# One pad for all pools, and the seven operands of the FFN's products at seven distances from the weights

## The chip, the cores and the metric

The kernel runs on one core of a Trainium2 chip. The metric is the device time of one execution in microseconds, the median of several runs. Profiled executions are looked at on the same core; times inside them count from the first instruction.

## What is computed

One layer of a streaming encoder on 512 tokens of width 1024, all in float32. A combined projection feeds three mixers and their gates, the gated branches are added and projected, and a gated feed-forward network (FFN) follows. The change touches memory placement in all of it, and code in the FFN alone:

```
D_MODEL, SEQ = 1024, 512
D_FF = 2816                       # 22 blocks of 128

h = rms_norm(x, norm_mix)
proj = h @ w_in                   # pool, LRU, q, k, v, three gates
...
merged = g0 * (y_pool @ w_branch[0]) + g1 * (y_lru @ w_branch[1]) + g2 * (y_sb @ w_branch[2])
x = x + merged @ w_out
h2 = rms_norm(x, norm_ffn)
act = silu(h2 @ w_ffn_gate) * (h2 @ w_ffn_up)
x = x + act @ w_ffn_down
```

## The kernel before

Every float32 product is made of three matmuls of a reduced-precision type (`float32r`): each operand is split into a high part (ScalarE copies it into the narrower type) and a low part (VectorE subtracts the high part from the original), and TensorE adds high x high, high x low and low x high (`mm3`, lines 215 to 218). A weights' chunk is loaded by a DMA issued on SP, split by `split_w` (lines 89 to 93) into tiles `whi` and `wlo`, three buffers each, and then used. TensorE loads 128x128 weights for every matmul, ahead of it, and streams the other ("moving") operand past them, 512 or 256 columns at a time.

The stages, with the tiles that the prediction names:

- gates, LRU and the q, k, v products: the moving operand of `half_chunk` (lines 264 to 272) is the normalised input `HH`, `HL`, in the pool `hp` on the right-hand side of the memory; in `tok_product` (line 654) the roles are exchanged, and `HH`, `HL` (or differences of them, on the left-hand side) are the weights
- the attention, whose tasks are dealt out between the matmuls of pool and branch chunks. Its products with 256 and 384 columns are `z` (scores) and `py` (lines 216 to 218 again)
- the output projection `ps_out`; its moving operand `mth`, `mtl` lies in the pool `cor`, on the right-hand side
- the FFN. Two of the eleven column chunks of gate and up are made directly (`ps_fg`, `ps_fu`). For the other nine, `seven(c)` replaces eight half-size products by seven (`product`, lines 1113 to 1121, matmuls at line 1119, 256 columns wide): the weights' blocks and their sums are named 11, 12, S2, S1, S3, S4, 22, and each goes with one of seven operands made from the activations: 11, 21, T2, T1, T3, 22, T4 (the table `WITH`). `split_b` (line 1040) makes an operand's high and low tile, `B0...`
- the down projection. Chunks kc = 4 to 10 of the activations are multiplied directly into `ps_d` (the loop with `split_act`, from line 1228); chunks 0 to 3 go through the seven products again, with operands `B1...`, made by `split_b` and `split2` (line 1204), into `ps_dy` and `ps_dx`

A pool's tiles with one tag share that tag's buffers in turn: a new tile waits until the last reader of the tile before it in the same buffer is done. In the FFN's pool `gp`, the tag "g" has 27 buffers of 4 KB per partition (`GBUFS`). They hold the eleven `act` tiles, the temporaries `tx`, `ty`, the split activations `ah`, `al`, sums, and the fourteen high and low tiles of the seven operands. Tiles of the constants' pool `cst` come first in memory, and the pools on the left-hand side follow it, so the size of `cst` shifts all of them.

The scheduler of the language orders the instructions of each engine from priorities and its own estimates; background tasks (`bg`) are emitted one by one between groups of matmuls.

Of the kernel before, what the change touches and what calls it, by code (L numbers as in the profile page):

```python
# [8 lines left out]
F32 = mybir.dt.float32  # L9
F32R = mybir.dt.float32r  # L10
# [6 lines left out]
P = 128  # L17
S = 512
# [7 lines left out]
QSCALE = float(HD) ** -0.5  # L26
NEG = -1.0e30
WARM = 8
GBUFS = 27
NDIRECT = 2  # L30
KD = 4
H = S // 2
AHEAD = 200
NAW, NAT, NAB = 8, 8, 13
NSP = 44
NLD = 12
# [24 lines left out]
def layer_kernel(ctx: ExitStack, tc: tile.TileContext, x, xt, vecs, w_in, w_pool, w_rg, w_ig,  # L61
# [5 lines left out]
    cst = ctx.enter_context(tc.tile_pool(name="cst", bufs=1))  # L67
# [131 lines left out]
    def emit_next():  # L199
# [4 lines left out]
        key, make = specs[i]  # L204
        with tc.high_priority(AHEAD if i > 3 else 0):
            ready[key] = make(str(i))
# [16 lines left out]
    def vcol(name, i=0):  # L223
        o = VOFF[name] + i
        return vt[:, o:o + 1]

    warm = cst.tile([P, S], BF16, tag="warm", name="warm")
    dve.memset(warm, 1.0)
    idn = cst.tile([P, P], F32, tag="idn", name="idn")
# [719 lines left out]
    for c in range(4):  # L949
        merge(2, c, chan_chunk(("br", 2, c), ysb_hl), g2[c])  # L950
        mth, mtl = corner([2, S], f"mth{c}", F32R), corner([2, S], f"mtl{c}", F32R)
        for j in range(2):
            h, l = mth[:, j, :], mtl[:, j, :]
# [7 lines left out]
    with ExitStack() as ffn:  # L961
        gp = ffn.enter_context(tc.tile_pool(name="gp", bufs=GBUFS))
        fp = ffn.enter_context(tc.tile_pool(name="fp", bufs=4, space=PSUM))

        def g4(shape, name, dt=F32):

            return gp.tile([P] + shape, dt, tag="g", name=name)
# [13 lines left out]
        for c in range(4):  # L981
# [5 lines left out]
            for j in range(2):  # L987
                k = 2 * c + j
                if c % 2 == 0:
                    x1p[c // 2, j] = mp.tile([P, 2, S], F32, tag="m", name=f"x1{c}{j}")  # L990
                t = x1p[c // 2, j][:, c % 2, :]
# [37 lines left out]
        B = {}  # L1029

        def norm2(k):
            for j in range(2):
                b = BN.setdefault((k // 4, j), None)
                if b is None:
# [2 lines left out]
                dve.scalar_tensor_tensor(b[:, k % 4, :], x1[k][:, js], vcol("norm_ffn", k),  # L1037
                                         rb2[:, js], ALU.mult, ALU.mult)

        def split_b(nm, key, which=0):  # L1040
            h, l = g4([4, H], f"B{which}{nm}h", F32R), g4([4, H], f"B{which}{nm}l", F32R)
            act(h, BN[key], AF.Copy)
            dve.tensor_tensor(l, BN[key], h.bitcast(F32), ALU.subtract)
            B[which, nm] = h, l
# [5 lines left out]
        def prepare_b():  # L1050
            nrm = [lambda k=k: norm2(k) for k in range(8)]
            return nrm[:4] + [lambda: split_b("11", (0, 0))] + nrm[4:] + [
                lambda: split_b("21", (1, 0)),
                lambda: diff_b("T1", (0, 1), (0, 0)),
                lambda: diff_b("T2", (1, 1), "T1"),
                lambda: split_b("T2", "T2"),
                lambda: split_b("T1", "T1"),
                lambda: diff_b("T3", (1, 1), (0, 1)),
                lambda: split_b("T3", "T3"),
                lambda: split_b("22", (1, 1)),  # L1060
                lambda: diff_b("T4", (1, 0), "T2"),
                lambda: split_b("T4", "T4")]
# [125 lines left out]
        for m in range(4):  # L1188
            t = fp.tile([P, 2, S], F32, tag="mm", name=f"ps_d{m}")
# [3 lines left out]
        def ablk(i, j):  # L1193
            return [acts[2 * i + n][:, :, j * H:(j + 1) * H] for n in range(2)]
# [7 lines left out]
            return [t[:, 0:2, :], t[:, 2:4, :]]  # L1202

        def split2(nm, i, j):
            h, l = g4([4, H], f"B1{nm}h", F32R), g4([4, H], f"B1{nm}l", F32R)
            for n, src in enumerate(ablk(i, j)):
                ns = slice(2 * n, 2 * n + 2)
                act(h[:, ns, :], src, AF.Copy)
                dve.tensor_tensor(l[:, ns, :], src, h[:, ns, :].bitcast(F32), ALU.subtract)
            B[1, nm] = h, l  # L1210

        todo = [lambda: load_a(DOWN), lambda: load_a(DOWN + 1),
                lambda: split2("11", 0, 0),
                lambda: split2("21", 1, 0),
                lambda: diff2("T1", ablk(0, 1), ablk(0, 0)),
                lambda: split_b("T1", "T1", 1),
                lambda: diff2("T2", ablk(1, 1), halves(BN["T1"])),
                lambda: split_b("T2", "T2", 1),
                lambda: diff2("T3", ablk(1, 1), ablk(0, 1)),
                lambda: split_b("T3", "T3", 1),  # L1220
                lambda: split2("22", 1, 1),
                lambda: diff2("T4", ablk(1, 0), halves(BN["T2"])),
                lambda: split_b("T4", "T4", 1)]
# [4 lines left out]
        for kc in range(KD, last + 1):  # L1228
            split_act(kc + 1)
            ah, al = split.pop(kc)  # L1230
            for e in range(2):
# [3 lines left out]
                for j in range(4):  # L1235
# [5 lines left out]
                    if kc == last:  # L1241
                        t = x1[m]
# [64 lines left out]
```

## Time and profile before

| | us |
|---|---|
| median of 3 runs | 957.63 (956.97 to 958.15) |
| the profiled execution | 956.69 |
| its span, first to last instruction | 954.9 |
| TensorE (PE) busy in the span | 941.5 |
| VectorE (DVE) busy | 703.5 |
| ScalarE (ACT) busy | 493.7 |

The granted clock of TensorE is 0.999 of full speed over the span. a tile's buffer number is left out of its name; PEld is the load of weights, which overlaps the matmul before it. [...] The chain of work that ended last is followed back from the last instruction; where TensorE is never idle, it is simply TensorE's own order. Instructions of VectorE and ScalarE on 128x1024 elements take 1.22 and 1.06 us, and follow each other at 1.14 and 0.95.

### The profile page before, as it was taken

The numbers are of one execution on the slowest core, as the hardware profiler recorded it, in microseconds if no ns is written. First come the engines' busy times: TensorE is split into PE (matmuls) and PEld (weight loads), VectorE is DVE, ScalarE is ACT, GpSimd is POOL, SyncE is SP. The second block draws the span as 40 slices with busy tenths as digits, with TensorE's granted clock in tenths as the row PEclk, the third lists the DMA queues.
The fourth block names the chain that finished last, engine by engine and source line by source line (L and its number), as shares of the span: only waits on it lengthen the run. The fifth ranks groups of instructions, "written<-read, shape, count | busy, mean of one in ns | idle before, by whom it ended". The sixth has DMA issues, their size and how long they took to land.

```text
span 954.9 us, 13025 instructions
## 1 busy us (share of the span) xinstructions
PE 941.5 (99%) x5090; PEld 802.7 (84%) x5090; DVE 703.5 (74%) x876; ACT 493.7 (52%) x664; POOL 43.1 (5%) x71
## 2 busy tenths in 40 slices
PE   8899999999999999999999999999999999999998
PEld 5787778788888888788788878889999999988898
DVE  6597677978696599865865554699888887787464
ACT  5567779445755466654543223555555555652232
POOL 1100000131121000000000000000000000000000
PEclk9999999999999999999999999999999999999999
DMA  8474343661713933165432234345533334523001
GB/s 269 138 260 130 111 136 129 199 204 58 224 65 138 297 117 121 63 178 165 146 101 88 89 114 153 108 122 145 150 93 89 111 95 129 166 98 111 1 27 63
DMA packets 127790, 124.12 MB, mean 130 GB/s; under 512 B 7280, under 2 KB 107632, under 8 KB 127728
## 3 DMA queue, kind: packets, MB, share of 16 engines
q1 hardware_dynamic: 123840, 109.13, 36.9%
q0 software_dynamic: 3888, 14.16, 4.4%
q8 instruction: 40, 0.66, 0.3%
q14 instruction: 22, 0.18, 0.1%
HBM read 107.01 MB, written 16.25 MB: 129 GB/s over the span
## 4 chain that ended last, share of the span: by engine, by line
PE 91%; DVE 5%; ACT 2%; DMA 1%; issue 1%; SPq 0%; POOL 0%; DVEq 0%; ACTq 0%; POOLq 0%
PE ps_y L1119 11%; PE ps_q L654 9%; PE ps_x L1119 8%; PE ps_br L216 4%; PE ps_br L218 4%; PE ps_br L217 4%; PE ps_gate L217 4%; PE ps_gate L218 4%; PE ps_gate L216 4%; PE ps_d L216 3%; PE ps_d L218 3%; PE ps_d L217 3%; PE ps_dy L1119 2%; PE ps_dx L1119 2%; PE ps_out L216 2%; PE ps_lru L217 2%
## 5 line engine op out<-in xcount | busy, mean ns | idle before, releaser
L92 ACT ACTIVATE whi<-raw 128x1024 fp32r<-128x1024 f32 x93 | 98.3, 1058 | 159.0 <-PE ps_br L217 44.8
L93 DVE TENSOR_TENSOR wlo<-raw,whi 128x1024 fp32r<-128x1024 f32 x93 | 113.6, 1221 | 78.7 <-ACT whi L92 74.2
L1109 ACT ACTIVATE wh_S<-w_S 128x1024 fp32r<-128x1024 f32 x44 | 46.6, 1061 | 58.7 <-PE ps_y L1119 27.2
L1110 DVE TENSOR_TENSOR wl_S<-w_S,wh_S 128x1024 fp32r<-128x1024 f32 x44 | 53.6, 1221 | 13.7 <-ACT wh_S L1109 13.6
L1109 ACT ACTIVATE wh<-w 128x1024 fp32r<-128x1024 f32 x33 | 35.0, 1060 | 50.8 <-issue 13.4
L93 DVE TENSOR_TENSOR wlo<-qw,whi 128x1024 fp32r<-128x1024 f32 x36 | 43.9, 1221 | 20.5 <-ACT whi L92 20.2
L1110 DVE TENSOR_TENSOR wl<-w,wh 128x1024 fp32r<-128x1024 f32 x33 | 40.3, 1222 | 18.9 <-ACT wh L1109 18.9
L92 ACT ACTIVATE whi<-qw 128x1024 fp32r<-128x1024 f32 x36 | 38.0, 1056 | 30.4 <-PE ps_q L654 17.1
L216 PE MATMUL ps_gate<-HH,whi 128*128 128x512 f32 x128 | 50.9, 397 | 0.0
L218 PE MATMUL ps_gate<-HH,wlo 128*128 128x512 f32 x128 | 50.8, 397 | 0.0
L217 PE MATMUL ps_gate<-HL,whi 128*128 128x512 f32 x128 | 50.7, 396 | 0.0
L216 PE MATMUL ps_d<-ah,whi 128*128 128x512 f32 x112 | 43.6, 391 | 0.0
L217 PE MATMUL ps_d<-al,whi 128*128 128x512 f32 x112 | 43.6, 389 | 0.0
L218 PE MATMUL ps_d<-ah,wlo 128*128 128x512 f32 x112 | 43.6, 389 | 0.0
L1097 DVE TENSOR_TENSOR w_S<-w,w 128x1024 f32<-128x1024 f32 x22 | 26.9, 1222 | 3.4 <-PE ps_d L217 2.9
L218 PEld LDWEIGHTS ps_gate<-HH,wlo 128*128 128x128 f32 x128 | 24.1, 188 | 5.8
L217 PEld LDWEIGHTS ps_gate<-HL,whi 128*128 128x128 f32 x128 | 24.1, 188 | 5.7
L216 PEld LDWEIGHTS ps_gate<-HH,whi 128*128 128x128 f32 x128 | 24.1, 188 | 5.6
L1097 DVE TENSOR_TENSOR w_S<-w,w_S 128x1024 f32<-128x1024 f32 x22 | 26.9, 1223 | 0.6
L872 DVE TENSOR_TENSOR_SCAN E<-K,zero 128x511 f32<-128x511 f32 (+3 forms) x32 | 25.5, 813 | 1.5 <-ACT K L867 1.3
L216 PE MATMUL ps_out<-mth,whi 128*128 128x512 f32 x64 | 25.4, 398 | 0.9 <-DVE g L299 0.9
L216 PE MATMUL ps_gate<-hu,whi 128*128 128x512 f32 x64 | 25.2, 394 | 1.0 <-ACT whi L366 0.7
(638 smaller groups left out, 3047.8 us busy)
## 6 DMA issues: line engine op xcount, KB each, us to landing
raw<-in_w_in_dram SPq DMA_DIRECT2D x39, 512.0 KB, 4.1
qw<-in_w_in_dram SPq DMA_DIRECT2D x24, 512.0 KB, 4.6
raw<-in_w_branch_dram SPq DMA_DIRECT2D x24, 512.0 KB, 3.4
w<-in_w_ffn_gate_dram SPq DMA_DIRECT2D x36, 256.0 KB, 3.5
w<-in_w_ffn_up_dram SPq DMA_DIRECT2D x36, 256.0 KB, 4.2
raw<-in_w_ffn_down_dram SPq DMA_DIRECT2D x14, 512.0 KB, 3.5
qd<-r POOLq DMA_DIRECT2D x12, 512.0 KB, 3.4
at<-qd SPq DMA_DIRECT2D x24, 256.0 KB, 5.2
```

What stands on the lines that cost most here:

```text
L92: act(hi, raw, AF.Copy)
L93: dve.tensor_tensor(lo, raw, hi.bitcast(F32), ALU.subtract)
L216: nc.tensor.matmul(ps, lh, rh, start=start, stop=False, skip_group_check=skip)
L217: nc.tensor.matmul(ps, lh, rl, start=False, stop=False, skip_group_check=skip)
L218: nc.tensor.matmul(ps, ll, rh, start=False, stop=stop, skip_group_check=skip)
L654: nc.tensor.matmul(ps[:, a, :], b_[:, k, ts_], a_[:, kk, :], start=first and n == k == 0, stop=n == 2 and k == 3, skip_group_check=True)
L872: dve.tensor_tensor_scan(E[:, f - 1:c0 + n - 1][:, ::-1], K[:, f:c0 + n][:, ::-1], zero[:, 0:1].to_broadcast([P, c0 + n - f]), 1.0, ALU.mu ...
L1097: dve.tensor_tensor(t, raw[c, x], raw[c, y], op)
L1109: act(h, raw[c, nm], AF.Copy)
L1110: dve.tensor_tensor(l, raw[c, nm], h.bitcast(F32), ALU.subtract)
L1119: nc.tensor.matmul(o, a[:, w, k, :], b[:, k, :], start=first and n == k == 0, stop=n == 2 and k == 3, skip_group_check=True)
```

## The change

A tile of 104 floats (416 B per partition) that nothing uses is added to `cst`. The seven operands get a tag each in `gp`, with one buffer that is used by `B0...` and then by `B1...`; high and low part lie in one tile of 8448 B, at an offset that is chosen per operand. "g" keeps 13 buffers. The offsets are such that each operand starts at the named number of bytes past the starts of the weights, modulo 512 B: 4 for 11, 256 for 21, 16 for T2, 320 for T1, 48 for T3, 384 for 22, 128 for T4.

```diff
-GBUFS = 27
+GBUFS = 13
...
+PAD = 104
...
+    cst.tile([P, PAD], F32, tag="pad", name="pad")
     warm = cst.tile([P, S], BF16, tag="warm", name="warm")
...
+        DIST = {"11": 4, "21": 256, "T2": 16, "T1": 320, "T3": 48, "22": 384, "T4": 128}
+        order = list(DIST)
+
+        def operand(which, nm):
+            n = order.index(nm)
+            o = (DIST[nm] - 256 * (n % 2)) // 4
+            assert 0 <= o <= 64
+            t = gp.tile([P, 2 * S * 2 + 64], F32R, tag="B" + nm, name=f"B{which}{nm}", bufs=1)
+            return [t[:, o + i * 1024:o + (i + 1) * 1024].rearrange("p (k t) -> p k t", k=4)
+                    for i in range(2)]
+
         def split_b(nm, key, which=0):
-            h, l = g4([4, H], f"B{which}{nm}h", F32R), g4([4, H], f"B{which}{nm}l", F32R)
+            h, l = operand(which, nm)
...
         def split2(nm, i, j):
-            h, l = g4([4, H], f"B1{nm}h", F32R), g4([4, H], f"B1{nm}l", F32R)
+            h, l = operand(1, nm)
```

In the built program the pad moves the starts of the left-hand tiles from 64 to 480, modulo 512 B; the right-hand pools stand at 480 before and after.

## The prediction

> **What bounds the kernel now.** I began with the page's first part: TensorE is busy all the time.
>
> ```profile
> span 954.9 us, 13025 instructions
> PE 941.5 (99%) x5090; PEld 802.7 (84%) x5090; DVE 703.5 (74%) x876; ACT 493.7 (52%) x664; POOL 43.1 (5%) x71
> ```
>
> So the end moves by what a matmul costs, and by what makes TensorE wait. Second, the table of busy time by stage (us, then PE, PEld, DVE, ACT, POOL, the granted clock, DMA). Look at the microseconds per matmul in the brackets of PE.
>
> ```profile
> 563.00:608.00 45.00, 44.73 (x191) 36.03 (x192) 21.69 (x28) 15.19 (x21) 0.00 (x0) 1.00 0.42 140
> ...
> 652.00:834.00 182.00, 182.00 (x1516) 181.92 (x1515) 150.70 (x138) 98.16 (x120) 0.00 (x0) 1.00 0.41 117
> 834.00:910.00 76.00, 76.00 (x337) 62.67 (x336) 51.98 (x56) 27.17 (x31) 0.00 (x0) 1.00 0.20 69
> ```
>
> The first and third rows hold the same matmul (128x512, weights 128x128, clock 1.00), `ps_out` and `ps_d`, yet 44.73/191 is 234 ns each and 76.00/337 is 226 ns. The middle row is the FFN's seven products: 182.00/1516 = 120 ns for 128x256. Third, the chain of work that ended last, where `ps_q` (L654) appears in groups:
>
> ```profile
> 157.68 11.20 PE ps_q L654 x48
> ...
> 231.59 5.45 PE ps_q L654 x24
> 237.05 5.44 PE ps_q1S L654 x24
> ...
> 253.54 5.60 PE ps_q1S L654 x24
> ```
>
> One line, one shape, two prices: 11.20/48 = 5.60/24 = 233 ns, and 5.45/24 = 227 ns. What sorts them is in the built program: where operands lie in a partition. "Distance" below is start of the moving operand minus start of the weights, modulo 512 B. The cheap groups are at distance 0 (both start 64 B past a multiple of 512), the dear `ps_q` groups at 96 (weights HH, HL at 480), `ps_out` at 416 (moving operand at 480, weights at 64). From start to start, waits left out (steps under 241 ns):
>
> - 1728 matmuls of 512 columns at distance 0: mean 227.6 ns, four in five at exactly 226 or 227, the rest, mostly the six or eight after an interruption, between 224 and 240
> - 960 at 416: mean 234.1, not one at 226 or 227; they repeat a cycle of seven steps from 231 to 238
> - 216 at 96: mean 233.3, a cycle of three
>
> So distance 0 lets the stream fall into a fixed step, and the other two do not. The 1848 matmuls of the seven products all stand at 0 and step by 120.
>
> **The change part by part.**
>
> *The pad* (104 floats in `cst`) moves every left-hand pool from 64 to 480, where the right-hand pools are. All 960 + 216 matmuls then stand at distance 0. At the mean of the rows that are there now: 960 x (234.1 - 227.6) + 216 x (233.3 - 227.6) = 6.2 + 1.2 = **-7.4 us**. It counts in full where TensorE sets the end, and their stages have it busy 98 to 100%. A stage in which VectorE came to end last would give its share back; the gate and LRU stage holds 382 of them, 2.5 us. Bounds: -8.8 (all at the fixed step of 226.7) to +10.5 (third rival).
>
> *The pool.* `gp` keeps 13 buffers under tag "g", not 27; the seven operands have their own. In the direct part of the down projection (L1228 on) the eleven `act` tiles and `ah4`, `al4` fill the 13. The built order of the changed kernel shows what follows: ScalarE's copy into `ah5` waits for the last matmul of kc=4, whose `ah4` it replaces, and the first matmul of kc=5 needs `ah5`. Before, `ah5` was ready 3.5 us early (ACT, L1175, 840.28, against 844.78). Call 844.78 T. ScalarE first does the weights' copy queued ahead of it (`whi`, 0.95 from start to start; its twin of the half before started at 839.32, with the matmul after its release), then `ah5` (1.04): T+2.0. VectorE's queue holds both halves of `act10` (0.60 each, now waiting for `al4`'s buffer), `wlo` (1.14) and only then `al5` (1.22): T+0.05+1.20+1.14+1.22 = T+3.6. TensorE has four matmuls that need `ah5` alone (0.9 us). It loses 2.05, runs 0.9, waits to 3.65: **+2.8 us**, with bounds +2.0 (VectorE not late) and +3.7 (no cover). What follows (`al6`, the operands of the second half) has 10.9 us per kc to be made in.
>
> *What else moves.* Two operands of the down products are split earlier, ahead of `wh10_S3` and `wh10_S4`: 2 x 0.57 on ScalarE and 2 x 0.64 on VectorE each, where ScalarE idles 1.3 to 1.9 us and VectorE 1.6 to 1.7 before each of those steps. `wl2_11` goes behind four `act0` steps on VectorE, from 645.5 to about 649, needed at 652.6. SP's DMAs keep their order; two loads of the first FFN chunk wait for another VectorE step, no later than theirs now. Nothing of this reaches TensorE; without the idle time each would cost up to 1.2 us.
>
> *The seven distances* (4, 256, 16, 320, 48, 384, 128; 264 matmuls each, 1848 in all) are the open term: no row shows any of them. What leaving the fixed step costs is known for 512 columns, +6.6 (at 96) and +7.4 (at 416). For 256 columns the nearest rows are the attention's products, distance 0 but too often interrupted to settle. Their starts:
>
> ```profile
> 408.25 0.28 PE L216 MATMUL py<-wth,vh 128*128 128x256 f32 x1
> 408.37 0.28 PE L217 MATMUL py<-wtl,vh 128*128 128x256 f32 x1
> 408.48 0.28 PE L218 MATMUL py<-wth,vl 128*128 128x256 f32 x1
> 408.60 0.28 PE L216 MATMUL py<-wth,vh 128*128 128x256 f32 x1
> 408.72 0.28 PE L217 MATMUL py<-wtl,vh 128*128 128x256 f32 x1
> 408.84 0.28 PE L218 MATMUL py<-wth,vl 128*128 128x256 f32 x1
> ```
>
> Five steps in 0.59 us: 118 ns, unsettled, and not above the settled 120. All 64 such matmuls (`z`, `py`) average 119.0, between 113 and 128, while unsettled ones of 512 columns at distance 0 average 232, 5 above their settled step. So at 256 columns an unsettled stream costs no more than a settled one. An odd distance cost 512 columns 1 to 2 ns beyond "unsettled"; half of that here gives about 119.5. I take **-1.0 us** (1848 x -0.5 ns). Bounds: 113 ns each, -12.9; +7.4 each, +13.7. I take the value near the first, the row of the same shape.
>
> *Sum.* Against the profiled execution (956.69: span 954.9 and 1.8 around it): 956.69 - 7.4 + 2.8 - 1.0 = 951.1. It lies 0.9 under the median of the runs (957.63), so I predict **952.0**, with a range of its own of 949 to 955.5.
>
> [...]
>
> **The rivals.**
>
> 1. *The price is per weight load (slower).* A weight load reads 128 columns whatever the matmul's width (PEld 188 ns beside 512 columns, 192 beside 256), and beside 256 columns it runs all the time (181.92 of 182 us). If the two reads get in each other's way once per load, the price of 512 columns holds: 1848 x 6.6 to 7.4 = +12.2 to +13.7. 957.6 - 7.4 + 2.8 + 13.0 = **966**. It decides from 2.5 ns a matmul on, where the FFN eats the rest of the gain. For: the settled steps 226.7 and 120.0 differ by 106.7 for 256 columns, which leaves the same 13.3 in both, so something is paid per matmul and load. Against: the 118 above.
> 2. *Some distances are as good as 0.* 416 and 96 are both 32 past a multiple of 64. If multiples of 64 settle (256, 320, 384, 128) and 4, 16 and 48 pay rival 1's price: 792 x 7 = 5.5, **958.5**. Nothing separates them before.
> 3. *Not the distance but the place counts.* Starts at 480 may be dear as such; then the pad gains nothing and makes the 1728 cheap matmuls dear: 1728 x 6.1 = +10.5, **971**. Against: with weights alone at 480 a load of 188 ns has room in a step of 227, and the price rose all the same.
> [...]
>
> **How the numbers follow.** My forecast 0.42; rival 1 0.27; rival 2 0.14; rival 3 0.06; rival 4 0.06; a real gain from unsettled streams (towards 113 ns, under 949) 0.05. From 948 to 967.5 the range leaves out rival 3, the deep gain and the top of rival 1, some 0.14. This kernel's measurement can tell about 0.2% (1.9 us) from no change. Faster: the forecast and the deep gain, 0.47. Same (955.7 to 959.5): most of rival 2, 0.12. Slower: rivals 1, 3, 4 and the rest of 2, 0.41.
>
> **What would show it.** The pad: `ps_out`'s 192 matmuls in about 43.7 us instead of 44.9, and all 24-groups of `ps_q` at 5.45. The pool: TensorE idle about 2 us before the first `ps_d` matmul of kc=5 and 0.7 four matmuls later, released by ScalarE `ah` and VectorE `al`. The distances: the groups of 24 in the chain stand at 2.88 each now; 2.85 would be my value, 3.05 rival 1, a split between operands (2.88 for 21, T1, 22 and T4, 3.05 for 11, T2 and T3) rival 2. I am wrong if the groups go over 2.94, or if `ps_d`, at distance 0 before and after, changes its 226.7.

## The result, and the profile after

The changed kernel takes 954.62 us (median of 7 runs, 953.60 to 955.76); the kernel before, beside it on the same chip, 958.15 (956.97 to 959.40). The ratio is 0.9964, with a 95% interval of 0.9953 to 0.9975: 3.5 us or 0.36% faster. The profiled execution took 955.76, its span 954.0; before, 956.69 and 954.9. So the two profiles differ by 0.9 us only, and the four parts of that difference are what has to be explained.

The first part of the page after (busy us and share of the span for each engine):

```profile
span 954.0 us, 13027 instructions
PE 937.0 (98%) x5090; PEld 803.7 (84%) x5090; DVE 703.0 (74%) x876; ACT 492.9 (52%) x664; POOL 43.0 (5%) x71
```

TensorE is busy 4.5 us less, the span is 0.9 shorter: 3.6 us of new idle time. The busy times by stage (start and end, us, then PE, PEld, DVE, ACT, POOL, the granted clock, DMA), for `ps_out`, the seven products and `ps_d`, as in the prediction:

```profile
562.50:606.10 43.60, 43.60 (x192) 36.12 (x193) 21.46 (x27) 14.92 (x21) 0.00 (x0) 1.00 0.43 145
650.30:830.40 180.10, 180.10 (x1514) 180.10 (x1513) 152.81 (x143) 99.47 (x124) 0.00 (x0) 1.00 0.41 118
830.40:906.80 76.40, 74.18 (x326) 60.58 (x325) 48.43 (x50) 25.09 (x25) 0.00 (x0) 1.00 0.21 69
```

`ps_out` has its 192 matmuls in 43.60 us (227 ns each, not 234). The seven products step by 180.10/1514 = 119.0 ns, not 120, and not all alike: in the chain of work (below: start, us, engine, tile, matmuls), 24 matmuls of any operand took 2.88 us before (first line), and after it is 2.85 for T2 and 2.83 for T1 (second and third). `ps_d` keeps its 74.18/326 = 227.5, but TensorE is idle for 2.2 us of the stage.

```profile
736.12 2.88 PE ps_x L1119 x24
...
736.29 2.85 PE ps_y L1134 x24
739.14 2.83 PE ps_x L1134 x24
```

The chain after also shows that `ps_q` has one price now, 5.44 for 24, in every group that no wait interrupts (behind a wait 5.70 and 5.73):

```profile
199.31 5.44 PE ps_q0S L657 x24
204.75 5.44 PE ps_q L657 x24
215.63 10.88 PE ps_q L657 x48
231.95 5.44 PE ps_q L657 x24
```

TensorE's waits from 830 to 860 us are the two that the prediction worked out, with ScalarE and VectorE as releasers:

```profile
PE ps_d L217 <- ACT ah L1190: 1.9, 1, 1.9
PE ps_d L218 <- DVE al L1191: 0.3, 1, 0.3
```

One thing was not foreseen. In the stretches 12 to 16 and 41 to 44 us of the trace after, the granted clock (third number from the end) falls to 0.62 and 0.56:

```profile
12.00:16.00 4.00, 4.00 (x11) 2.89 (x11) 3.73 (x13) 3.45 (x5) 0.00 (x0) 0.62 0.91 292
...
41.00:44.00 3.00, 3.00 (x11) 2.48 (x11) 2.10 (x3) 0.52 (x1) 0.00 (x0) 0.56 0.00 0
```

The kernel before has 1.00 in both, and 18 and 15 matmuls where these rows have 11 each. When the starts of all matmuls are laid side by side, matmul by matmul, the difference after minus before is +4.05 us at matmul 180 (50 us into the span). From there the pad's stages bring -6.24 (50 to 652 us), the nine chunks of seven products -1.31, kc=4 and 5 of the down projection +2.82, the down products -0.25. Together -0.93, the difference of the spans.

### The profile page after: what moved, and what is told of

Same layout as the page of the kernel before. It is cut to its first block, busy times and chain, and to the rows that moved or that the text cites. A ratio compares the mean times of both kernels' runs of the same rounds, so it can differ in the third digit from the quotient of the medians.

```text
span 954.0 us, 13027 instructions
## 1 busy us (share of the span) xinstructions
PE 937.0 (98%) x5090; PEld 803.7 (84%) x5090; DVE 703.0 (74%) x876; ACT 492.9 (52%) x664; POOL 43.0 (5%) x71
## 4 chain that ended last, share of the span: by engine, by line
PE 88%; DVE 6%; ACT 2%; issue 1%; DMA 1%; POOL 1%; SPq 0%; DVEq 0%; POOLq 0%; ACTq 0%
PE ps_y L1134 11%; PE ps_x L1134 8%; PE ps_q L657 7%; PE ps_br L217 4%; PE ps_br L219 4%; PE ps_br L218 4%; PE ps_gate L218 4%; PE ps_gate L217 4%; PE ps_gate L219 4%; PE ps_d L218 3%; PE ps_d L219 3%; PE ps_d L217 3%; PE ps_dy L1134 2%; PE ps_dx L1134 2%; PE ps_out L217 2%; PE ps_out L218 2%
## 5 line engine op out<-in xcount | busy, mean ns | idle before, releaser
L1134 PE MATMUL ps_y<-B0T,wh_S 128*128 128x256 f32 x288 | 52.1, 281 | 0.0
L1134 PEld LDWEIGHTS ps_y<-B0T,wh_S 128*128 128x128 f32 x288 | 44.2, 188 | 0.0
L1134 PE MATMUL ps_y<-B0T,wl_S 128*128 128x256 f32 x144 | 40.4, 281 | 0.0
```

The lines of the kernel that those rows point to most:

```text
L1134: nc.tensor.matmul(o, a[:, w, k, :], b[:, k, :], start=first and n == k == 0, stop=n == 2 and k == 3, skip_group_check=True)
```

## The experiments

My theory after this comparison: four separate terms, of which three are the prediction's (pad, pool wait, distances) and the fourth, at the start, is TensorE waiting for transfers and then running at half clock. The rivals: the start belongs to the pad's addresses; or the start is chance; or the steps of the seven products go with the operand and not with the distance. Each was timed beside the kernel before on the same chip:

| kernel | us, median | ratio to before (95%) | granted clock of its runs |
|---|---|---|---|
| pad_left | 951.43 | 0.9928 (0.9914 to 0.9943) | 0.996 to 1.000 |
| pad_right | 951.39 | 0.9925 (0.9911 to 0.9939) | 0.997 to 1.000 |
| dist_zero | 956.69 | 0.9978 (0.9968 to 0.9989) | 0.994 to 0.998 |
| nowait | 950.30 | 0.9919 (0.9904 to 0.9934) | 0.995 to 1.000 |
| changed_again | 955.11 | 0.9962 (0.9946 to 0.9977) | 0.995 to 0.998 |
| half_wait | 955.65 | 0.9971 (0.9958 to 0.9985) | 0.994 to 0.998 |
| all_320 | 949.03 | 0.9891 (0.9872 to 0.9911) | 0.996 to 1.000 |
| seven_more | 949.60 (one run) | - | 0.998 |
| all_64 | 949.19 | 0.9905 (0.9890 to 0.9919) | 0.996 to 0.998 |
| pad_64 | 953.17 | 0.9947 (0.9934 to 0.9960) | 0.997 to 0.999 |
| alt_32_64 | 943.91 | 0.9853 (0.9836 to 0.9870) | 0.998 to 1.000 |
| one_32 | 946.03 | 0.9871 (0.9846 to 0.9897) | 0.996 to 0.998 |

The kernel before had medians of 958.05 to 958.68 beside them, and clocks of 0.996 to 1.000.

**The pad alone (pad_left).** The kernel before with one added tile:

```diff
+    cst.tile([P, PAD], F32, tag="pad", name="pad")
     warm = cst.tile([P, S], BF16, tag="warm", name="warm")
```

> The kernel before with the pad of 104 floats alone, 27 shared buffers, all matmuls at distance 0. From the two traces: 1176 matmuls of 512 columns gain 6.2 us from 50 us into the span on, the first 50 us lose 4.0. My theory, that both belong to the pad: 958.15 - 6.2 + 4.0 = 956.0 us, granted clock 0.996 to 0.998, half-clock matmuls (step 427 ns) some 13 and some 40 us into the span. Rival, that the loss at the start comes with the FFN's new tiles or by chance: 952, clock 0.999.

Measured: 951.43, 7.2 us under the kernel before; 956.0 was wrong and the rival's 952 right. The profile has the clock at 0.999, its start 0.13 us behind that of before at matmul 180, and a span of 948.9, 6.0 less. So the pad does not cost the start anything.

**The pad on the other side (pad_right).**

```diff
+    rpad = ctx.enter_context(tc.tile_pool(name="rpad", bufs=1, side="right"))
+    rpad.tile([P, 104], F32, tag="rpad", name="rpad")
     hp = hstack.enter_context(tc.tile_pool(name="hp", bufs=1, side="right"))
```

> The kernel before with the 104 floats put into a pool on the right-hand side instead: left-hand tiles stay at 64, right-hand tiles move from 480 to 64, all distances are 0 as with the pad on the left. Theory A, that DMAs that land at 480 (32 past a multiple of 64) come later and TensorE's clock falls in the waits: the start stays as before, 958.15 - 6.2 = 952.0 us, clock 0.999. Rival, that the loss at the start comes with distance 0 itself (the first stage's matmuls were at 416 before) or from anything but the landing address: 956, clock 0.996 to 0.998. Rival 3 of the prediction (the place 480 counts) would make this kernel faster than the left pad in the FFN too.

Measured: 951.39, the same as the pad on the left. Left tiles at 64 or at 480, landings at 64 or at 480: no difference. But this profile lost 1.2 us at 38 us into the span, with the clock at 0.87 there, which theory A excluded. Both theories on addresses are dead, and so is the prediction's rival 3 (the place 480). TensorE waits 1.7 to 4.3 us for `rbps` at about 36 us in all 14 traces, and in 11 of them the clock then falls to half, for 3.41 us in nine and 6.83 in two. The profile of before was one of the three without it, that of after lost the clock twice. The start is no part of the change.

The records of the clock in the traces also show what went with such a fall. Within one trace, all changes of the clock lie whole multiples of 3.413 us apart, as on a grid: in that of after the clock is half from 12.94 to 16.36 us and from 40.25 to 43.66, with 23.89 us (seven times 3.413) of full clock between. Between 20 us and the last matmul of the 14 traces, TensorE was idle for 1.86 us or more in 14 stretches of that grid at full clock, and half clock followed all 14; the least of them are 1.86 us (36.84 to 40.25 in after, and one at 184 us in all_320). No full-clock stretch with less was followed by it. The kernel before waited 2.78 us for `rbps`, but the grid cut the wait in two, with 1.78 us idle in the longer part, and its clock stayed. So it did in after at 841 us, where the grid cut a wait of 1.92 us into 0.94 and 0.98. In these traces, what differs is where the grid lies against a wait. No run was made to test this reading, and two falls in the first 13 us (after, all_320) came behind less idle time, 1.55 and 1.22 us.

**The distances taken out (dist_zero).**

```diff
-        DIST = {"11": 4, "21": 256, "T2": 16, "T1": 320, "T3": 48, "22": 384, "T4": 128}
+        DIST = {"11": 0, "21": 0, "T2": 0, "T1": 0, "T3": 0, "22": 0, "T4": 0}
...
-            o = (DIST[nm] - 256 * (n % 2)) // 4
+            o = (DIST[nm] - 256 * (n % 2)) % 512 // 4
```

> The changed kernel with all seven operands at distance 0. If the seven distances are worth what the traces show (steps of 117.8 to 122.3 ns, mean 119.2, against 120.0), this takes 1.5 us more than the changed kernel, 956.1, and all 1848 matmuls step by 120.0. Rival, that another part of the change (fewer buffers, other tiles) moved those steps: 954.6, steps as in the changed kernel.

Measured: 0.9978 against the changed kernel's 0.9964, 1.3 us more (the intervals overlap), and all seven operands back at 120.0 ns. The distances are worth 1.6 us, by the steps (1848 x 0.84 ns). This profile also shows what a wait can bring behind it (stretches around the first matmuls of kc=5, columns as above):

```profile
840.00:843.00 3.00, 1.08 (x5) 0.67 (x4) 3.00 (x4) 2.93 (x3) 0.00 (x0) 0.96 0.00 0
843.00:846.00 3.00, 2.96 (x8) 1.97 (x7) 2.86 (x4) 0.00 (x0) 0.00 (x0) 0.50 0.50 175
846.00:850.00 4.00, 4.00 (x19) 3.29 (x18) 1.38 (x2) 1.20 (x2) 0.00 (x0) 0.98 0.00 0
```

TensorE is idle 1.9 us in the first row; in the second it has the half clock for 3 us and starts 8 matmuls. Here kc=4 and 5 lose 4.04 us, not 2.8.

**The pool's wait taken out (nowait).** ah5 and al5 go into T4's tile:

```diff
-                h, l = g4([2, S], f"ah{kc}", F32R), g4([2, S], f"al{kc}", F32R)
+                if kc == KD + 1:
+                    t = gp.tile([P, 2 * S * 2 + 64], F32R, tag="BT4", name=f"ahl{kc}", bufs=1)
+                    h, l = [t[:, i * 1024:(i + 1) * 1024].rearrange("p (k t) -> p k t", k=2)
+                            for i in range(2)]
+                else:
+                    h, l = g4([2, S], f"ah{kc}", F32R), g4([2, S], f"al{kc}", F32R)
```

> The changed kernel with the split activations of kc=5 (ah5, al5) in the tile of operand T4, which is free from the end of the nine chunks until its second use, so that ScalarE and VectorE need not wait for kc=4. If the pool's wait is what the trace shows, 2.8 us go: 954.6 - 2.8 = 951.8. Rival, that the wait only moves (to ah6 or to T4's second making): 954.6.

Measured: 950.30. TensorE has no wait left between 825 and 860 us, and nothing appears elsewhere. The ratio moves from 0.9964 to 0.9919, 4.3 us. That is more than the 2.8 us of idle time, but the two intervals together leave 2.5 to 6.1 us, so 2.8 alone is not excluded.

**The changed kernel again (changed_again).** No edit.

> The changed kernel itself, beside the others of this call. Theory W, that the wait at kc=5 costs 2.8 us and in part of the executions lets the clock fall to half for up to 3.4 us after it: the granted clock of its runs averages about 0.002 less than that of the kernel before, and its ratio to the kernel before is again 0.996 to 0.998. Rival S, that the clock falls by chance at the start only and as often in every kernel: the clocks of both kernels scatter alike, and the ratio comes to 0.994 (954.9 - 7.5 + 2.8 - 1.5 + ... = some 6 us under before).

Measured: 0.9962, as first measured. The granted clock of the 31 runs of kernels with the wait (seven_more's one left out) averages 0.9957, of the 43 runs of kernels without it 0.9979, and of 50 runs of the kernel before 0.9982. So the sign is theory W's, and the 0.994 of rival S did not come. How much of it belongs to the wait is less clear: the 12 runs of the changed kernel itself average 0.9964 and the six of nowait 0.9972, which is 0.7 us of 955, and the two traces of the changed kernel have their half clock at the start, none behind kc=4. Of five traces with the wait, two (dist_zero, half_wait) show it there, so the price is 2.8 us in some executions and 4 or more in others. By the grid of 3.413 us above, the changed kernel's two waits (1.92 and 0.30 us) bring 1.86 us, the least that half clock followed, into one stretch in 56% of the positions that the grid can have; at the 1.2 us that it cost in dist_zero (4.04 - 2.82), that makes 0.7 us on average. This is an estimate.

**Half of the wait (half_wait).** ah5 alone in T4's tile:

```diff
...
+                    h = t[:, 0:1024].rearrange("p (k t) -> p k t", k=2)
...
+                l = g4([2, S], f"al{kc}", F32R)
```

> The changed kernel with ah5 alone in the tile of operand T4; al5 is in a shared buffer as before. If the prediction's working is right (VectorE's queue, act10 behind al4's buffer, then wlo, then al5, ends last), TensorE now runs its four first matmuls of kc=5 at once and then waits 2.7 us in one piece for al5: nothing is gained, 954.6. Rival, that the wait on ScalarE's copy sets the price: 2.0 us less, 952.6.

Measured: 955.65, nothing gained. The timeline of TensorE has the four matmuls at once and then one wait, on VectorE:

```profile
839.53 1.07 PE L217 MATMUL ps_d<-ahx,whi 128*128 128x512 f32 x4
843.13 0.50 PE L218 MATMUL ps_d<-al,whi 128*128 128x512 f32 x1 [2.52 <-DVE al L1196]
```

VectorE's queue ends last, as worked out. A longer single wait (2.5 us) was followed by the half clock from 844 to 847 us, and kc=5 lost 4.4 us in all.

**All operands at 320 (all_320).** No wait; tiles chained so that each starts at the distance wanted:

```diff
+            o = (DIST[nm] - phase) % 512
...
+            phase = (phase + n) % 512
...
+        DIST = {"11": 320, "21": 320, "T2": 320, "T1": 320, "T3": 320, "22": 320, "T4": 320}
```

> The changed kernel without the wait (ah5 and al5 in T4's tile, at distance 0) and with all seven operands at distance 320. If the distance sets the step, all 1848 matmuls take the 117.8 ns that T1 has at 320: 1848 x (119.2 - 117.8) = 2.6 us less than the kernel without the wait at seven distances (950.3): 947.7. Rival, that the place in the order of the products or the operand sets the step: each operand keeps its own mean (11 122.3, 21 119.4, T2 119.1, T1 117.8, T3 118.3, 22 and T4 118.5), 950.3.

Measured: 949.03, and 117.8 ns for every operand, 117.77 to 117.87. Here the distance sets the step, and the operand does not. (This profile stood 2.2 us behind before at matmul 60 and had a second clock drop at 186 us, so its total is less clear than its steps.)

**Seven more distances (seven_more).** The same chain with 8, 32, 64, 192, 288, 448, 320 for 11, 21, T2, T1, T3, 22, T4; the wait is in.

> The changed kernel (with the wait) with seven other distances: 8 for 11, 32 for 21, 64 for T2, 192 for T1, 288 for T3, 448 for 22, 320 for T4. If the distance sets the step, T4 now steps by 117.8 as T1 did, and 11 leaves its 122.3; the other steps are not foreseen by any theory beyond 113 to 123 ns. If the operand sets it, each keeps its mean.

Measured, mean steps in ns: 8: 119.8; 32: 116.9; 64: 113.5; 192: 117.8; 288: 116.8; 448: 114.3; 320: 117.8. T4 at 320 has T1's price. In one chunk of the chain of work (start, us, engine, tile, matmuls), the second to the sixth operand:

```profile
730.13 2.81 PE ps_x L1144 x24
732.94 2.72 PE ps_y L1144 x24
735.66 2.83 PE ps_x L1144 x24
738.49 2.80 PE ps_y L1144 x24
741.29 2.73 PE ps_x L1144 x24
```

The third and sixth products, at 64 and 448, take 2.72 and 2.73 us: 113.3 and 113.8 ns, beneath every group of 256 columns before; only single steps of the attention come as low. The mean at 448 holds two steps, 117.8 in the first chunk and 113.9 in the other eight. With the wait and a clock drop at the start, this one run took 949.6.

**All at 64 (all_64),** the cheapest, without the wait:

> The changed kernel without the wait and with all seven operands at distance 64, which stepped by 113.5 ns for T2 in the kernel with seven more distances. If the distance alone sets the step, 1848 x (117.8 - 113.5) = 7.9 us less than all at 320 (949.0): 941. Rival, that the cheap step needs neighbours at other distances (T2's products come between others): the steps go back to 117 to 120 and the time stays at 949 to 953.

Measured: 949.19; the rival was right. The chain:

```profile
734.36 2.83 PE ps_y L1144 x24
737.18 2.83 PE ps_x L1144 x24
740.01 2.83 PE ps_y L1144 x24
```

2.83 for 24 everywhere: 117.8 again, at the distance that had 113.5 in the kernel before it. Distance alone does not set the step.

**All operands behind the weights at 64 (pad_64).** The kernel before with small pads on both sides, 64 B behind the weights' pool among them:

```diff
+    lpad = ctx.enter_context(tc.tile_pool(name="lpad", bufs=1))
+    lpad.tile([P, 16], F32, tag="lpad", name="lpad")
+    rpad = ctx.enter_context(tc.tile_pool(name="rpad", bufs=1, side="right"))
+    rpad.tile([P, 88], F32, tag="rpad", name="rpad")
...
+    cor.tile([P, 16], F32, tag="cpad", name="cpad", bufs=1)
```

> The kernel before (27 shared buffers, no wait) with 64 B between the weights' pool and all left-hand pools behind it, and 352 B on the right: every operand of the seven products is at 64, and of the 2914 matmuls of 512 columns 2066 go from 0 or 416 to 64, 504 to 448 and 336 stay at or go to 0. If 64 is a cheap distance for 512 columns too, by the same 6.5 ns a matmul, these give 2570 x 6.5 = 16.7 us beyond the seven products' 12: 951.4 - 12.1 - 16.7 = 923. If 512 columns gain nothing over the settled 226.7: 939. If 64 is as dear for them as 96 and 416 are (233 to 234): 939 + 2570 x 7 = 957.

Measured: 953.17, between the cases. 512 columns take 229.5 ns at 64 (2066 matmuls), 233.4 at 448 (504), and 227 to 228 at 0: for them 0 is the best distance seen. The nine chunks stand at 117.8, but the down products, still at 64, at 2.72/24 = 113.3, for all seven operands:

```profile
911.41 2.72 PE ps_dx L1124 x24
914.13 2.72 PE ps_dy L1124 x24
916.85 2.72 PE ps_dx L1124 x24
```

In all_64 the same products at the same distance take 2.83. One distance, two settled steps. The difference between the two kernels is the stream ahead: 512 columns at 64 here, 512 columns at 0 there. It can't be all: the nine chunks of this kernel also come behind 512 columns at 64 (`ps_fg` and `ps_fu`, 229 ns), and they took 117.8.

**32 and 64 in turn (alt_32_64), and 32 once (one_32).** Both are all_64 with another table; shown is that of alt_32_64 against all_64's. one_32 has 32 for 11 and 64 for the rest.

```diff
-        DIST = {"11": 64, "21": 64, "T2": 64, "T1": 64, "T3": 64, "22": 64, "T4": 64}
+        DIST = {"11": 32, "21": 64, "T2": 32, "T1": 64, "T3": 32, "22": 64, "T4": 64}
```

> The changed kernel without the wait, with distances 32 for 11, 64 for 21, 32 for T2, 64 for T1, 32 for T3, 64 for 22 and T4. Theory H, that at 64 the stream can lock at 113.3 or at 117.8 and that which one it takes is set by the stream it enters from (113.5 behind an operand at 32 that never locks, 117.8 behind operands at 64 that do): 32 takes 116.9, 64 takes 113.5 in four operands, mean 114.9, and the time is all_64's 949.2 less 1848 x (117.8 - 114.9) = 5.3: 944. Rival, that the 113.5 came from something else in the kernel with seven more distances: 64 stays at 117.8, 949.

Measured: 943.91, theory H's 944, though not by its steps alone. Their mean is 115.5 ns (115.1 in the nine chunks, 117.2 in the down products), which makes 4.2 of the 5.3 us under all_64; the granted clock of the runs also averages 0.9992, against 0.9970 in all_64. In the chain the products alternate, and those at 64 take 2.72, or 113.3 ns a matmul:

```profile
728.36 2.72 PE ps_x L1144 x24
731.08 2.81 PE ps_y L1144 x24
733.89 2.72 PE ps_x L1144 x24
736.62 2.81 PE ps_y L1144 x24
739.43 2.72 PE ps_x L1144 x24
```

> The same with operand 11 alone at 32 and the six others at 64. By theory H and if a lock is kept from one operand to the next of the same distance, six operands take 113.3, mean 113.9, and the time is 949.2 - 1848 x (117.8 - 113.9) = 942. Rival, that a lock at 113.3 doesn't outlast the change of operand: 21 at 113.5, the others back at 117.8, mean 117.0, 947.7.

Measured: 946.03, with runs in two groups, 942.2 to 943.8 and 948.3 to 949.4. The profiled run is of the first; all operands behind 11 stay at 2.72 in eight of its nine chunks:

```profile
731.20 2.72 PE ps_y L1144 x24
733.91 2.72 PE ps_x L1144 x24
736.63 2.72 PE ps_y L1144 x24
```

In its first chunk the T1 group was interrupted (24 matmuls in 3.2 us), and the operands after it stood at 117.8 until 11 came round again. So in this trace the lock at 113.3 outlasted a change of operand, and an interruption ended it. That the runs near 949 are such losses in every chunk is my guess; no trace shows them. And theory H is not the whole: in the down products of both kernels the operands at 64 behind 32 took 117.9, where in those of seven_more the operand at 64 behind 32 took 113.5. What picks the lock beyond the stream ahead stays open. alt_32_64, which enters the lock three times a chunk, is the fastest kernel by its median and steadier (942.9 to 945.9): 1.5% under the kernel before, 1.1% under the changed one.

## Why the prediction came out right, and where its steps were off

The forecast was 952.0, or -5.6 from a median of 957.63; measured were 954.62 and -3.5 (-2.4 to -4.5 by the interval), inside the range of 949 to 955.5 and near its upper end. The mechanisms of the pad and of the pool were the right ones. For the distances the direction was right, the reason given for it was not, and the size is in good part luck. The terms one by one:

- **The pad, -7.4.** Its matmuls gained a little more than was said (234.1 and 233.3 ns before, 227.0 after, where the prediction took 227.6). In the traces 6.0 us arrive (pad_left; 6.2 in the changed kernel from 50 us on), by medians 7.2 with an interval of 5.5 to 8.2, so that only the traces show a shortfall. The step that was off by them is "it counts in full where TensorE sets the end". The gates and the LRU gave all of it (346 matmuls, 2.33 us), `ps_out` too (1.41), but the stretch of the q, k, v products (148 to 289 us) gave 1.21 of about 2.3 and the one from there to 413 us 1.17 of about 1.7. In the first of these TensorE came earlier and waited longer: its steps over 241 ns, the waits and the slow starts behind them, take 1.4 us more than before. What ate the rest in the second is not shown. The bound of -8.8 is -8.5 by the prediction's own means (960 x 7.4 + 216 x 6.6). The waits of `ps_q`, before and with the pad alone:

```profile
PE ps_q L654 <- ACT r L666: 1.3, 1, 1.3
```

```profile
PE ps_q L656 <- ACT r L668: 1.8, 1, 1.8
...
PE ps_q L656 <- DVE wlo L94: 0.2, 1, 0.2
```

- **The pool, +2.8.** In the trace 2.07 us ahead of the first matmul of kc=5 and 0.74 after the fourth, 2.81 together; half_wait shows that VectorE's queue sets it. What was missing from the term is the half clock that can follow: dist_zero and half_wait lost 4.0 and 4.4 us at this place, over the upper bound of 3.7 ("no cover"). What it adds in the changed kernel on average stays open; the estimate above is 0.7 us, and nowait's gain of 4.3 us fits it but does not prove it.
- **Other moves, 0.** Right: in pad_left and nowait no new wait appears in the FFN.
- **The distances, -1.0.** Measured -1.6 (-1.31 in the nine chunks, -0.25 below). The seven means run from 117.8 (320) to 122.3 (4), and only 4 is dearer than 0. Taking the attention's row of the same width as the nearest was right. The reason given for it was not: 320 is as settled as 0, in a cheaper cycle (117.8 ns in all_320, 120.0 in dist_zero), and "distance 0 lets the stream fall into a fixed step, and the other two do not" holds for 512 columns at 0, 96 and 416 alone. Other sets of distances gave means from 114.8 (one_32) to 120.0 ns (dist_zero), so that this set came out near the forecast's 119.5 is in good part luck. The groups of operand 11 took 2.94 us (24 x 122.3), at the very edge of the sign of being wrong, "over 2.94".
- **The rivals.** Rival 1 needed 2.5 ns a matmul on top; the mean fell by 0.84. Rival 2's split is not there (48 has 118.3, 256 has 119.4). Rival 3 fell with pad_left and pad_right, which took the same time with the left-hand tiles at 480 and at 64. Rival 4, that no distance counts (the pool's +2.8 alone, 960.4), would have left pad_left at the time of before; it was 0.9928 of it.
- **The base.** The profile of before had a better clock at its start (0.999) than its runs on average (0.998), so adding 0.9 us for the median was too little: beside the result, the median of before is 1.5 us over its profile. Of the 2.6 us between forecast and result, the largest pieces are the pad's shortfall (7.4 less 6.0 to 6.2, 1.2 to 1.4 by the traces), the half clock behind the wait (some 0.7, the estimate) and the base (0.5); the distances gave 0.6 back. What is left is no more than the scatter of the runs (953.60 to 955.76).

## What to carry to other kernels

Look at the time from start to start of equal matmuls by operand address (in the trace after, a 512-column matmul's own record is 0.39 us long, and the next starts 0.23 us after its start): where one shape has several prices, the offset of the moving operand against the weights is worth trying, shape by shape, and a good offset has to be tried in its sequence, since one offset had two settled steps (113.3 and 117.8 ns at 64), and what streamed ahead had a part in which of them came. A gain in TensorE's steps counts only as far as the stage's other engines follow: here the stretch of the q, k, v products gave 1.21 of about 2.3 us. A wait of 2 us on TensorE is to be priced with the half clock that can come behind it: behind the 1.9 us in dist_zero kc=4 and 5 lost 4.04 us, not 2.82; from 20 us on, it came in these traces where 1.86 us or more of idle time fell into one stretch of 3.41 us. Profiles of two kernels are to be compared by stage and granted clock before a difference at the start is put down to the change.

## What the hardware showed unexpectedly

- At 256 columns and distance 64 there are two settled steps, 113.3 and 117.8 ns, at distance 0 a third, 120.0. Which of the first two is taken went with what streamed before in the nine chunks of all_64, alt_32_64 and one_32, but not in the down products of the last two. It can persist for hundreds of matmuls (113.3 in nearly all 336 of the down products of pad_64).
- At 512 columns the order is another: by means of steps under 241 ns, 0 has 227.2 (the kernel after), 64 229.5 and 448 233.4 (pad_64), 96 233.3 and 416 234.1 (before).
- Idle times of TensorE of 1.86 us (38 us into the trace after), 1.92 (841 in dist_zero) and 1.86 (184 in all_320) were followed by 3.41 us at a granted clock of one half; waits as long or longer stayed without it where the grid of 3.41 us cut them in two (2.78 us in before, 1.92 in after).
